# A factor for each position: spread over the partitions by a product, or read back from DRAM as one row

## The chip, the cores and the metric

The kernel runs on one core of a Trainium2 chip. Its engines are TensorE (PE in the profile, with PEld for its weight loads), VectorE (DVE), ScalarE (ACT) and GpSimd (POOL); SyncE (SP) issues most of the transfers. The metric is the device time of one launch in microseconds, lower is better.

## The reference

One layer of a hybrid block on x of 2048 positions by 1024 channels, in float32:

```python
h = rms_norm(x, norm1_g)                      # x * rsqrt(mean(x*x) + eps) * g
proj = h @ w_in                               # [u_a | v_a | val_b | gate_b], 512 columns each
u, v = gelu(u_a), layer_norm(gelu(v_a))
a = u * (tril(W_s[head]) @ v + b)             # within chunks of 128 positions
g = val_b * sigmoid(gate_b)
c = silu(group_layer_norm(causal_depthwise_conv31(g)))
x = x + concat([a, c]) @ w_out
f = square(relu(rms_norm(x, norm2_g) @ w_ff1))
x = x + f @ w_ff2
return rms_norm(x, final_g)
```

There are three root mean square norms. In each of them one factor per position, rsqrt(mean + eps), multiplies all 1024 channels of that position.

## The kernel before

**Layout.** Activations lie with channels on the 128 partitions and positions along the row: a piece of one block of 512 positions is a tile of 128 x 512, and eight such pieces are the 1024 channels. There are four blocks. Every large product is made as three (`mm3`): each float32 operand is split into a high part (rounded, by ACT: `h_hi`, `w_hi`, `fo_hi`) and a low part (the rest, by POOL or DVE: `h_lo`, `w_lo`, `fo_lo`), and hi x hi, hi x lo and lo x hi are added in one PSUM bank.

**Stages.** The order is "vgvgvgovgooo". `stage_v` makes the columns of u and v (`pvv`, `pu`) with their gating product (`sgu`); `stage_g` makes val and gate (`pv`, `pg`), and their `g<-pv,sg` starts a convolution on DVE: `conv_chain`, 31 steps `acc<-g,vec,acc` into PSUM, of which the last writes `c` into SBUF. `conv_tail` follows: PE transposes `c` (`ct`), DVE takes statistics of it (`st`, `mv`, `nb`, `ve`), POOL raises them to the power, ACT normalises, PE transposes back (`cb`). `stage_o` is the output projection (`po`). Then come the first layer of the MLP (`px`, `py`, `pz`; a Strassen-like set of seven products over blocks), the second (`py` with `fo` and `w2o`), 16 chunks for each pair of blocks, and the last norm with the output (`finish` for blocks 0 and 1, `finish_third`, `finish_last`).

**The factors.** The sum of squares of a block comes with positions on partitions, as a tile of 128 x 4 (`ss`), DVE adds eps (`ve`), and POOL raises to the power -1/2 (`r`, or `r1`). But the factors are needed as a row of 512, the same on all 128 partitions. `spread` makes that by a product. DVE multiplies the identity by `r`, which gives `dg`, four diagonal blocks side by side, and PE multiplies a matrix of ones by it, into a PSUM bank (`rbc`). The product has float32 operands and appears as two records in the trace. There are 13 of them:

- block 0's first norm (1), where the row is used after the projection;
- `make_h` for blocks 1 to 3 (3): DVE scales the eight pieces of the input `hf`, which SP loads, by gain and factor, reading the factor from the PSUM bank (`hf<-hf,vec,rbc`), then ACT and POOL split them. `make_h(b+1)` is a generator in the queue that `stage_g(b)` moves on by `tick`;
- `row_scale` for blocks 0 to 3, the second norm (4): one beat after the sums the power is taken, then `dg`, one beat later the product, one beat later ACT copies the bank into `r_rows`, a tile that the first MLP layer reads;
- `finish` for blocks 0 and 1 (2), eight DVE steps `x<-x,vec,rbc` with an output transfer each; one for the third block and two for the last.

**What sets the order.** The program is recorded by the Python code with clocks of its own (`dve.time`, `pe.time`); `background` puts convolution steps on DVE while its clock lags. `later(n, f)` calls f after n beats, a beat being half of an output column of `stage_o`. A scheduler then orders the instructions of the early stages, with pools whose buffers come free when the last reader has finished: `ct`, `cb`, `rbc`, `sgu` share the PSUM pool `tp`. `stage_o` and the MLP's first layer are kept in the written order. SP executes its queue in order, and so a transfer that waits holds those behind it.

Of the kernel before, what the change touches and what calls it, by code (L numbers as in the profile page):

```python
# [9 lines left out]
F32 = mybir.dt.float32  # L10
# [3 lines left out]
ALU = mybir.AluOpType  # L14

P = 128
# [3 lines left out]
TB = 512  # L20
KD = D // P
# [5 lines left out]
V_G1, V_G2, V_LNG, V_LNB, V_CB, V_CG, V_CBE = 0, 8, 16, 20, 24, 28, 32  # L27
V_FG = 36
# [54 lines left out]
def hybrid_block_kernel(  # L83
# [14 lines left out]
    nc = tc.nc  # L98
    dve = Clocked(nc.vector, lambda n: 0.35 if n <= 128 else 0.17 + n / 960.0)
    dcv = Clocked(nc.vector, lambda n: 0.15 + n / 960.0, dve.clock)  # L100
    dsb = Clocked(nc.vector, lambda n: 0.22 + n / 512.0 if n <= 512 else n / 640.0, dve.clock)
    gps = Clocked(nc.gpsimd, lambda n: 0.35 + n / 488.0 if n > 8 else 1.1)
    pe = Clocked(nc.tensor, lambda n: 0.0135 + n / 2400.0)
    pe4 = Clocked(nc.tensor, lambda n: 0.0135 + n / 600.0, pe.clock)
# [3 lines left out]
    dram = ctx.enter_context(tc.tile_pool(name="dram", bufs=1, space=bass.MemoryType.DRAM))  # L108
# [17 lines left out]

    p_d = dram.tile([2, 4, P, 2, TB], F32, name="p_d")
    x1_d = dram.tile([NB, 4, P, 1024], F32, name="x1_d")
    f_d = [dram.tile([8, 4, P, 2, TB], F32, name=f"f_d{i}") for i in range(2)]
    w2_d = dram.tile([8, 7, 2, P, 2, 512], F32, name="w2_d")  # L130
    w1_d = dram.tile([2, 7, P, 2, 512], F32, name="w1_d")
# [8 lines left out]
    def tmp(name, dtype=F32):  # L140
        return t2.tile([P, 512], dtype, tag="tmp", name=name)

    def bank(kind, name):
        return banks[kind].tile([P, 512], F32, tag=kind, name=name)

    def mm_tile(name):
        return bank("mm", name)

    def tp_tile(name):
        return bank("tp", name)  # L150

    def tiny(name, n=4):
        return small.tile([P, n], F32, tag=f"{name}{n}", name=name)

    def act_pair(name):
        return slot(f"{name}_hi", F32R), slot(f"{name}_lo", F32R)

    def split(src, hi, lo):

        nc.scalar.copy(hi, src)  # L160
        rest(src, hi, lo)
# [13 lines left out]
    def halves(pair):  # L175
        return [(pair[0][:, a * 512:a * 512 + 512], pair[1][:, a * 512:a * 512 + 512])
                for a in range(2)]
# [58 lines left out]
    ones = const.tile([P, P], F32, name="ones")  # L236
# [12 lines left out]
    def v(off, j):  # L249
        return vec[:, off + j:off + j + 1]  # L250

    def rsqrt(dst, src, mul):
        n = dst.shape[1]
        ve = tiny("ve")
        dve.tensor_scalar(ve[:, :n], src, mul, EPS, op0=ALU.mult, op1=ALU.add)
        gps.tensor_tensor(dst, ve[:, :n], nhalf.to_broadcast([P, n]), op=ALU.pow)
# [149 lines left out]
    def norm1(b, r):  # L406

        ss = tiny("ss")
        xin = []

        def load(i):
            xin.append(slot("xin"))
            nc.sync.dma_start(xin[i], x[(4 * b + i) * P:(4 * b + i + 1) * P, :])

        load(0)
        for i in range(4):
            if i < 3:
                load(i + 1)
            yield
            junk = t2.tile([P, 1024], BF16, tag="tmp", name="junk")  # L420
            nc.scalar.activation(junk, xin[i], AF.Square, accum_out=ss[:, i:i + 1])
        rsqrt(r, ss, 1.0 / D)

    def spread(r, ps):

        dg = tmp("dg")
        n = r.shape[1]
        dsb.tensor_tensor(
            dg.rearrange("p (n t) -> p n t", t=P)[:, :n, :],
            ident.unsqueeze(1).to_broadcast([P, n, P]),  # L430
            r.unsqueeze(2).to_broadcast([P, n, P]), op=ALU.mult)
        yield
        pe4.matmul(ps, ones, dg[:, :n * P], start=True, stop=True)

    def make_h(b, h):
        r = tiny("r1")
        yield from norm1(b, r)
        yield
        ps = tp_tile("rbc")
        yield from spread(r, ps)  # L440
        hf = []

        def load(k):
            hf.append(tmp("hf"))
            nc.sync.dma_start(hf[k], xt[b, k // 2, :, k % 2, :])

        load(0)
        for k in range(KD):
            if k < KD - 1:
                load(k + 1)  # L450
            yield
            if k % 2 == 0:
                pair = halves(act_pair("h"))
            dve.scalar_tensor_tensor(
                hf[k], hf[k], v(V_G1, k), ps, op0=ALU.mult, op1=ALU.mult)
            split(hf[k], *pair[k % 2])
            h.append(pair[k % 2])

# [31 lines left out]
    def feature_sums(acc, n, pc=None):  # L490

        pc = tp_tile("ssum") if pc is None else pc
        for i in range(n):
            for k, sq in enumerate(acc):
                pe4.matmul(pc[:, i:i + 1], sq[:, i * P:(i + 1) * P], ones[:, 0:1],
                           start=k == 0, stop=k == len(acc) - 1)
        return pc[:, :n]
# [100 lines left out]
    def later(n, f, first=False):  # L598
        due.append([n, f, first])
# [25 lines left out]
    def row_scale(b):  # L625

        r = r2[b]

        def spread_out():
            ps = tp_tile("rbc")  # L630
            g = spread(r, ps)
            next(g)

            def product():
                next(g, 0)
                later(1, lambda: nc.scalar.copy(r_rows[:, b % 2, :], ps))
            later(1, product)

        def sums():
            ps = feature_sums(acc[b], 4)  # L640
            later(1, lambda: rsqrt(r, ps, 1.0 / D))
            later(2, spread_out)
        return sums

    r_rows = const.tile([P, 2, TB], F32, name="r_rows")
# [40 lines left out]
    for kp in range(1, 4):  # L686
# [10 lines left out]
        out=wt, in_=wt, pattern=[[0, 4], [1, P]], compare_op=ALU.is_ge, fill=0.0,  # L697
# [47 lines left out]
    queue.append(make_cbias())  # L745
    late, rows0 = stage_v(0, h[0], parts[0], r0)
    queue.append(make_h(1, h[1]))
    stage_g(0, h[0], parts[0], late, rows0)
    drain()
    late, _ = stage_v(1, h[1], parts[1])  # L750
    queue.append(make_h(2, h[2]))
    slow.append(first_units())
    stage_g(1, h[1], parts[1], late)
    drain()
    late, _ = stage_v(2, h[2], parts[2])
    queue.append(split_mix(parts[0], mix[0]))
    queue.append(load_resids(0))
    stage_g(2, h[2], parts[2], late)
    drain()
    queue.append(make_h(3, h[3]))  # L760
    dve.time += BEHIND
    with tc.manual_schedule():
        stage_o(0, lambda d: tick(1))
    drain()
    late, _ = stage_v(3, h[3], parts[3])
# [212 lines left out]
    def up_out(pair):  # L978
        kept = {}

        def out(m, i, ps):
            blk_ = INTO[i]
            def copy():
                kept[m, blk_] = tmp("c")
                nc.scalar.copy(kept[m, blk_], ps)  # L985

            def finish():
                if i == 4:
                    src, c = ps, tmp("c")
                else:  # L990
                    c = kept.pop((m, blk_))
                    src = c if i == 7 else ps
                    dve.tensor_tensor(src, ps, c, op=ALU.add)
                (dsb if i == 7 else dve).scalar_tensor_tensor(
                    c, src, 0.0, r_rows[:, blk_[1], :], op0=ALU.max, op1=ALU.mult)
                later(1, lambda: nc.scalar.activation(c, c, AF.Square))  # L996
                later(2, lambda: nc.scalar.dma_start(
                    f_d[pair][m // 2, 2 * blk_[0] + blk_[1], :, m % 2, :], c))

            later(1, copy if i in (1, 5, 6) else finish, True)  # L1000
        return out
# [65 lines left out]
    with tc.manual_schedule():  # L1067
        stage_o(2, at_o2)
        pace["w2"] = 0.0
        k = w2st.at[2]  # L1070
# [4 lines left out]
    dn = {"x": [[] for _ in range(NB)]}  # L1075
# [53 lines left out]
    def finish(b, acc):  # L1129

        gaps = (6, 3, 4)
        for _ in range(gaps[0]):
            yield
        r = tiny("r1")
        ve = tiny("ve")
        ps = feature_sums(acc, 4, mm_tile("ssum"))
        yield
        dve.tensor_scalar(ve, ps, 1.0 / D, EPS, op0=ALU.mult, op1=ALU.add)
        gps.tensor_tensor(r, ve, nhalf.to_broadcast([P, 4]), op=ALU.pow)
        for _ in range(gaps[1]):  # L1140
            yield
        dg = tmp("dg")
        times_ident(dg, r)
        for _ in range(gaps[2]):
            yield
        ps = mm_tile("rbc3")
        pe4.matmul(ps, ones, dg, start=True, stop=True)
        x = dn["x"][b]
        for k in range(KD):
            yield  # L1150
            dve.scalar_tensor_tensor(x[k], x[k], v(V_FG, k), ps, op0=ALU.mult, op1=ALU.mult)
            nc.sync.dma_start(out[b, k // 2, :, k % 2, :], x[k])

    def times_ident(dg, r):
        dsb.tensor_tensor(
            dg.rearrange("p (n t) -> p n t", t=P), ident.unsqueeze(1).to_broadcast([P, 4, P]),
            r.unsqueeze(2).to_broadcast([P, 4, P]), op=ALU.mult)

    def gained(x, ks):
        for k in ks:  # L1160
            nc.scalar.activation(x[k], x[k], AF.Copy, scale=v(V_FG, k))
# [232 lines left out]
```

## Time and profile before

| | |
|---|---|
| median of 3 runs | 1819.01 us (1817.65 to 1820.26) |
| profiled execution | 1819.57 us |
| its span | 1817.8 us, mean granted clock 0.998 |
| PE busy | 1805.2 us, 99% |
| DVE busy | 1318.6 us, 73% |
| ACT busy | 754.6 us, 42% |
| POOL busy | 1232.4 us, 68% |

A row of the timeline has the start, the duration in us, the engine, the line and operation, the output and the inputs by their names, partitions x elements, and how many like it follow one another; in brackets stands the idle time before it and what ended that. The rows of L78 are those of a helper through which all DVE, POOL and PE operations are recorded, so they are told apart by the names of their tiles. Of three numbers in a row on a tile, the first to the third are the least, the median and the largest duration in ns.

### The profile page before, as it was taken

What the parts mean: (1) busy time and instruction counts of PE and PEld (TensorE: products, weight loads), DVE (VectorE), ACT (ScalarE), POOL (GpSimd) and SP (SyncE); (2) the same over time, 40 slices, a digit from 0 to 9 for tenths busy, and PEclk for the clock granted to TensorE, in tenths of its full rate; (3) what the DMA queues carried; (4) which work ended last, traced back from release to release, by engine and by line L of the source; (5) the groups of instructions that cost most, each with busy time, mean ns of one, the idle gap of its engine ahead of it and who ended that gap; (6) DMA issues with size and microseconds to landing.
All of it is one profiled execution on the core that took longest, in us unless ns stands there. A gap on an engine that the chain in (4) does not pass through costs nothing.

```text
span 1817.8 us, 23247 instructions
## 1 busy us (share of the span) xinstructions
PE 1805.2 (99%) x8080; PEld 1488.0 (82%) x8080; DVE 1318.6 (73%) x1832; ACT 754.6 (42%) x1170; POOL 1232.4 (68%) x788
## 2 busy tenths in 40 slices
PE   9999999999999999999999999999999999999998
PEld 7888888888888888888888888888888887888886
DVE  4699997996898985532667787787766678665565
ACT  6435556454454454455455555433212131222112
POOL 4575986884766666699778989786756464444434
PEclk9999999999999999999999999999999999999999
DMA  8353637442645464685557778999987679777752
GB/s 337 107 173 101 222 135 272 163 145 81 231 152 180 161 215 179 224 298 207 189 191 276 271 255 298 354 401 382 357 350 262 255 259 336 297 240 259 254 185 93
DMA packets 131686, 424.74 MB, mean 234 GB/s; under 512 B 14576, under 2 KB 15216, under 8 KB 131568
## 3 DMA queue, kind: packets, MB, share of 16 engines
q1 hardware_dynamic: 96000, 329.12, 50.7%
q10 hardware_dynamic: 35568, 94.13, 13.2%
q8 instruction: 64, 1.05, 0.2%
q14 instruction: 54, 0.44, 0.1%
HBM read 302.60 MB, written 120.59 MB: 233 GB/s over the span
## 4 chain that ended last, share of the span: by engine, by line
PE 92%; DVE 6%; issue 1%; POOL 1%; DMA 0%; ACT 0%; POOLq 0%; SPq 0%; DVEq 0%; ACTq 0%
PE py L78 51%; PE pz L78 9%; PE po L78 9%; PE px L78 5%; PE pv L78 4%; PE pg L78 4%; PE pu L78 4%; PE pvv L78 4%; DVE acc L78 3%; PE sgu L78 1%; PE rbc L78 0%; PE ssum L78 0%; DMA raw<-in_w_o 0%; PE cb L78 0%; PE ct L78 0%
## 5 line engine op out<-in xcount | busy, mean ns | idle before, releaser
L78 PE MATMUL py<-fo_hi,w2o 128*128 128x512 f32 x1792 | 555.1, 390 | 1.0 <-DVE x L78 1.0
L78 POOL TENSOR_TENSOR fo_lo<-fraw,fo_hi 128x1024 fp32r<-128x1024 f32 x112 | 283.0, 2535 | 260.6 <-ACT fo_hi L160 231.1
L78 DVE TENSOR_TENSOR x<-py,x 128x512 f32<-128x512 f32 x448 | 299.9, 687 | 175.4 <-PE py L78 175.2
L78 PEld LDWEIGHTS py<-fo_hi,w2o 128*128 128x128 f32 x1792 | 336.4, 188 | 71.6 <-DVE x L78 1.4
L78 PE MATMUL py<-hop,w1o 128*128 128x512 f32 x1536 | 363.6, 390 | 0.5 <-ACT c L985 0.5
L78 PE MATMUL py<-fo_lo,w2o 128*128 128x512 f32 x896 | 348.6, 389 | 0.0
L78 PEld LDWEIGHTS py<-hop,w1o 128*128 128x128 f32 x1536 | 287.7, 188 | 62.0 <-issue 1.3
L78 DVE SCALAR_TENSOR_TENSOR acc<-g,vec,acc 128x512 f32<-128x512 f32 x464 | 324.4, 750 | 1.9
L160 ACT CAST fo_hi<-fraw 128x1024 fp32r<-128x1024 f32 x112 | 116.9, 1052 | 424.7 <-PE py L78 209.7
L78 POOL TENSOR_TENSOR w_lo<-raw,w_hi 128x1024 fp32r<-128x1024 f32 (+1 forms) x94 | 224.1, 2390 | 61.4 <-ACT w_hi L160 50.9
L78 POOL TENSOR_TENSOR w1o<-wraw,w1o 128x512 fp32r<-128x512 f32 x120 | 172.9, 1446 | 51.9 <-ACT w1o L813 42.0
L78 PEld LDWEIGHTS py<-fo_lo,w2o 128*128 128x128 f32 x896 | 168.2, 188 | 35.6 <-issue 0.7
L78 PE MATMUL pz<-hop,w1o 128*128 128x512 f32 x768 | 183.8, 390 | 0.0
L78 POOL TENSOR_TENSOR w1o<-ws,w1o 128x512 fp32r<-128x512 f32 x90 | 128.9, 1435 | 65.4 <-ACT w1o L813 60.3
L78 PEld LDWEIGHTS pz<-hop,w1o 128*128 128x128 f32 x768 | 143.8, 188 | 29.7
L78 DVE TENSOR_TENSOR fraw<-fraw 128x1024 f32<-128x1024 f32 x64 | 92.1, 1439 | 16.3 <-POOL fo_lo L78 14.3
L996 ACT ACTIVATE c<-c 128x512 f32<-128x512 f32 x128 | 80.8, 632 | 54.8 <-DVE c L78 54.2
L78 PE MATMUL po<-m_hi,w_hi 128*128 128x512 f32 x256 | 101.1, 395 | 0.0
L78 PE MATMUL po<-m_hi,w_lo 128*128 128x512 f32 x256 | 99.9, 390 | 0.6 <-POOL w_lo L78 0.6
L78 PE MATMUL po<-m_lo,w_hi 128*128 128x512 f32 x256 | 99.7, 389 | 0.0
L78 DVE TENSOR_TENSOR px<-px,c 128x512 f32<-128x512 f32 x32 | 22.4, 699 | 102.3 <-PE px L78 69.0
L78 POOL TENSOR_TENSOR w2p<-wraw,w2p 128x512 fp32r<-128x512 f32 x64 | 92.6, 1447 | 2.6 <-ACT w2p L813 2.6
(157 smaller groups left out, 2928.4 us busy)
## 6 DMA issues: line engine op xcount, KB each, us to landing
w2o<-w_d SPq DMA_DIRECT2D x224, 512.0 KB, 6.2
w_d<-w2p ACTq DMA_DIRECT2D x112, 512.0 KB, 5.0
wraw<-in_w SPq DMA_DIRECT2D x92, 512.0 KB, 4.6
f_d<-c ACTq DMA_DIRECT2D x128, 256.0 KB, 4.0
fraw<-f_d SPq DMA_DIRECT2D x64, 512.0 KB, 6.7
raw<-in_w_ct SPq DMA_DIRECT2D x48, 512.0 KB, 5.2
raw<-in_w_o SPq DMA_DIRECT2D x32, 512.0 KB, 5.9
w1o<-w_d SPq DMA_DIRECT2D x28, 512.0 KB, 5.5
```

Of the source, the lines that this page charges most:

```text
L78: return op(out, *args, **kwargs)
L160: nc.scalar.copy(hi, src)
L996: later(1, lambda: nc.scalar.activation(c, c, AF.Square))
```

## The change

Nine of the thirteen products, those of `make_h`, `row_scale` and `finish`, are replaced by two transfers on SP's queue: `write_factor` puts `r` (128 x 4 floats) into a row of 512 in DRAM, and `read_factor` reads this row back to all 128 partitions (256 KB). `make_h` and `finish` read the result from an SBUF tile `rows`, `row_scale` reads straight into `r_rows`. In `finish`, POOL multiplies two of the eight pieces, to which ACT gave the gain first, and the output transfers are issued two steps later.

```diff
+    r_d = dram.tile([9, 4, P], F32, name="r_d")
...
+    def write_factor(n, r):
+        nc.sync.dma_start(r_d[n].rearrange("n p -> p n"), r)
+
+    def read_factor(n, rows):
+        nc.sync.dma_start(rows, r_d[n].rearrange("n p -> (n p)").unsqueeze(0).to_broadcast([P, TB]))
...
     def make_h(b, h):
         r = tiny("r1")
         yield from norm1(b, r)
         yield
-        ps = tp_tile("rbc")
-        yield from spread(r, ps)
+        write_factor(5 + b, r)
+        yield
+        rows = tmp("rows")
+        read_factor(5 + b, rows)
         hf = []
...
             dve.scalar_tensor_tensor(
-                hf[k], hf[k], v(V_G1, k), ps, op0=ALU.mult, op1=ALU.mult)
+                hf[k], hf[k], v(V_G1, k), rows, op0=ALU.mult, op1=ALU.mult)
...
     def row_scale(b):
-        def spread_out():
-            ps = tp_tile("rbc")
-            g = spread(r, ps)
-            next(g)
-
-            def product():
-                next(g, 0)
-                later(1, lambda: nc.scalar.copy(r_rows[:, b % 2, :], ps))
-            later(1, product)
-
         def sums():
             ps = feature_sums(acc[b], 4)
             later(1, lambda: rsqrt(r, ps, 1.0 / D))
-            later(2, spread_out)
+            later(2, lambda: write_factor(b, r))
+            later(4, lambda: read_factor(b, r_rows[:, b % 2, :]))
         return sums
...
     def finish(b, acc):
...
-        dg = tmp("dg")
-        times_ident(dg, r)
+        write_factor(4 + b, r)
+        gained(dn["x"][b], (0,2))
+        for _ in range(gaps[1]):
+            yield
+        rows = tmp("rows")
+        read_factor(4 + b, rows)
         for _ in range(gaps[2]):
             yield
-        ps = mm_tile("rbc3")
-        pe4.matmul(ps, ones, dg, start=True, stop=True)
         x = dn["x"][b]
-        for k in range(KD):
+        for k in range(KD + 2):
             yield
-            dve.scalar_tensor_tensor(x[k], x[k], v(V_FG, k), ps, op0=ALU.mult, op1=ALU.mult)
-            nc.sync.dma_start(out[b, k // 2, :, k % 2, :], x[k])
+            if k in (0,2):
+                gps.tensor_tensor(x[k], x[k], rows, op=ALU.mult)
+            elif k < KD:
+                dve.scalar_tensor_tensor(
+                    x[k], x[k], v(V_FG, k), rows, op0=ALU.mult, op1=ALU.mult)
+            if k > 1:
+                nc.sync.dma_start(out[b, k // 2 - 1, :, k % 2, :], x[k - 2])
```

The scheduler lays out the early stages anew. Three places are shown. The first is DVE while block 1's `stage_g` runs, around the last step (`c`) of one convolution; `mv`, `nb`, `ve` are the statistics of an earlier one, `hf` are block 2's inputs. Before, with the eighth `hf` behind that `c`:

```order
L78 SCALAR_TENSOR_TENSOR acc<-g,vec,acc 128x512
L78 BN_AGGR mv<-st 128x2 x3
L78 TENSOR_TENSOR g<-pv,sg 128x512
L78 BN_AGGR mv<-st 128x2
L78 SCALAR_TENSOR_TENSOR acc<-g,vec,acc 128x512 x2
L78 TENSOR_SCALAR nb<-mv 128x4
L78 TENSOR_SCALAR ve<-mv 128x4
L78 SCALAR_TENSOR_TENSOR acc<-g,vec,acc 128x512
L78 SCALAR_TENSOR_TENSOR c<-g,vec,acc 128x512
L78 SCALAR_TENSOR_TENSOR acc<-g,vec,acc 128x512
L78 TENSOR_SCALAR acc<-g,vec 128x512
L78 SCALAR_TENSOR_TENSOR hf<-hf,vec,rbc 128x512
```

After, on the same engine, from the third of the new `hf` steps to that same `c`:

```order
L78 SCALAR_TENSOR_TENSOR hf<-hf,vec,rows 128x512 x2
L78 SCALAR_TENSOR_TENSOR acc<-g,vec,acc 128x512
L78 SCALAR_TENSOR_TENSOR hf<-hf,vec,rows 128x512 x2
L78 TENSOR_TENSOR g<-pv,sg 128x512
L78 SCALAR_TENSOR_TENSOR acc<-g,vec,acc 128x512
L78 SCALAR_TENSOR_TENSOR hf<-hf,vec,rows 128x512
L78 SCALAR_TENSOR_TENSOR acc<-g,vec,acc 128x512 x6
L78 SCALAR_TENSOR_TENSOR hf<-hf,vec,rows 128x512
L78 SCALAR_TENSOR_TENSOR c<-g,vec,acc 128x512
```

All eight `hf` steps of the block now stand ahead of this `c`, the first two of them just above these rows; before, seven did. Counted over the stretch from the `g` ahead of the norm (at 171.10 us in the profile) to that `c`, 25 operations of 128 x 512 and a `dg` have become 29 and none.

PE at the start of `stage_v` for block 2, where `ct` are the transposes of that `c`. Before, they stand among the later `pvv` products:

```order
L78 MATMUL pvv<-w_hi,h_hi 128x512 x4
L78 MATMUL cb<-ident,c 128x128 x4
L78 MATMUL ct<-ident,c 128x128 x4
L78 MATMUL pvv<-w_lo,h_hi 128x512
L78 MATMUL pvv<-w_hi,h_lo 128x512
```

After, they follow the first three:

```order
L78 MATMUL pv<-h_hi,w_lo 128x512
L78 MATMUL pvv<-w_hi,h_hi 128x512 x3
L78 MATMUL ct<-ident,c 128x128 x4
L78 MATMUL pvv<-w_lo,h_hi 128x512
L78 MATMUL pvv<-w_hi,h_lo 128x512
```

They moved forward by some 75 products. On SP, around the same norm, before:

```order
L445 DMA hf<-in_xt 128x512 x3
L743 DMA w_d<-w1o 128x1024
L445 DMA hf<-in_xt 128x512 x4
L206 DMA raw<-in_w_v 128x1024 x2
L743 DMA w_d<-w1o 128x1024
```

and after:

```order
L438 DMA r_d<-r_1403 128x4x1
L745 DMA w_d<-w1o 128x1024
L442 DMA rows<-r_d 128x512
L456 DMA hf<-in_xt 128x512 x7
L207 DMA raw<-in_w_v 128x1024 x2
```

The three `hf` loads that stood ahead of a write of MLP weights (`w_d<-w1o`) now stand behind it and behind the factor's way through DRAM.

## The prediction

> **What bounds the kernel now.** I read the page first: the busy times, the slices, and the chain that ended last.
>
> ```profile
> span 1817.8 us, 23247 instructions
> PE 1805.2 (99%) x8080; PEld 1488.0 (82%) x8080; DVE 1318.6 (73%) x1832; ACT 754.6 (42%) x1170; POOL 1232.4 (68%) x788
> ...
> DVE  4699997996898985532667787787766678665565
> ...
> POOL 4575986884766666699778989786756464444434
> ...
> PE 92%; DVE 6%; issue 1%; POOL 1%; DMA 0%; ACT 0%; POOLq 0%; SPq 0%; DVEq 0%; ACTq 0%
> ```
>
> PE is busy 99% of the span and makes 92% of the chain. So a product that leaves PE shortens the run by its own length, unless PE then waits for somebody. The candidate stands in the slices: one slice is 45 us, and in slices 3 to 6 DVE is at 90% and more, with POOL at 50 to 90%. The windows of block 2's norm and of what follows it, and the chain in them, show who leads there:
>
> ```profile
> 171.00:198.00 27.00, 27.00 (x123) 22.05 (x122) 26.90 (x43) 13.81 (x21) 21.14 (x18) 1.00 0.72 238
> 198.00:259.00 61.00, 60.02 (x280) 49.33 (x278) 60.57 (x96) 38.46 (x55) 59.26 (x42) 1.00 0.53 191
> ...
> 198.31 17.12 DVE acc L78 x26
> ...
> 220.31 5.35 DVE nb L78
> ...
> 258.36 0.60 DVE u L78
> 259.10 1.13 PE sgu L78 x8
> ```
>
> Columns of a window are its length, then the busy times of PE, PEld, DVE, ACT and POOL. DVE is busy 87.47 of 88 us, and the chain runs on DVE until the `sgu` product at 259.10. Whatever DVE is given or spared between 171 and 259 us reaches the end one for one. Elsewhere PE leads.
>
> **The nine products.** What one of them costs PE is read from a pair of neighbours in block 3's norm, against the usual step of 24 products in 5.44 us, 0.227 us each:
>
> ```profile
> 89.80 5.44 PE pg L78 x24
> ...
> 303.98 0.40 PE L78 MATMUL po<-m_hi,w_lo 128*128 128x512 f32 x1
> 304.21 1.02 PE L78 MATMUL rbc<-dg,ones 128*128 128x512 f32 x2
> 304.67 0.80 PE L78 MATMUL po<-m_hi,w_hi 128*128 128x512 f32 x1
> 305.31 0.40 PE L78 MATMUL po<-m_lo,w_hi 128*128 128x512 f32 x1
> ...
> L78 PE MATMUL rbc<-dg,ones x26: 592/592/1069, 35.2 to 1809.5; 128*128 128x512 f32 x26
> ```
>
> From 303.98 to 305.31 are 1.33 us for two `po` steps and one `rbc` (two records): 1.33 - 2 x 0.227 = 0.874. The tile has 26 records, 13 products; block 0's, the third's and the last's two stay, so nine go: 9 x 0.874 = **-7.87 us**. The four ACT copies of `row_scale` go too, but no row has PE waiting for ACT there: zero.
>
> **Block 2's first norm.** The factor is now read from SBUF, where before it came from PSUM. The same operation stands in the trace in both forms (ns, least, median and most):
>
> ```profile
> L78 DVE SCALAR_TENSOR_TENSOR hf<-hf,vec,rbc x24: 733/744/748, 83.3 to 320.0; 128x512 f32<-128x512 f32 x24
> L78 DVE SCALAR_TENSOR_TENSOR c<-c,r_rows x32: 691/694/2708, 503.8 to 1174.2; 128x512 f32<-128x512 f32 x32
> L78 DVE SCALAR_TENSOR_TENSOR c<-c,r_rows 128x512 f32<-128x512 f32 x32 | 33.3, 1040 | 1.3
> L78 DVE SCALAR_TENSOR_TENSOR xr<-xr,vec 128x512 f32<-128x512 f32 x24 | 28.6, 1207 | 25.3 <-POOL hop L78 25.0
> 171.71 2.23 DVE L78 TENSOR_TENSOR dg<-ident,r 128x512 f32<-128x512 f32 x1
> ...
> 170.98 2.40 POOL L78 TENSOR_TENSOR w_lo<-raw,w_hi 128x1024 fp32r<-128x1024 f32 x1
> ```
>
> With one operand in PSUM the step takes 733 to 748 ns, never more; with both in SBUF it goes from 691 to 2708 ns, and its mean is 1040. The last two rows show why: `dg`, with both operands in SBUF, starts at 171.71 and is held until 173.9, just after POOL's `w_lo` ends at 173.38. DVE waits out whatever POOL has running.
>
> By the Trainium skill (SBUF — State Buffer, the rule on the shared port pair) the lock is exclusive for a whole instruction and the loser blocks. The trace agrees, in the 2.23 above. The rule speaks against this change: by it each `hf` step that finds POOL at work pays, and the eight of block 2 alone bring the sum from 1811.6 to 1816.8; by the row of 733 to 748 ns they would stay free.
>
> The price of one step therefore lies between 0 (POOL idle) and 2.4 (a whole `w_lo`); the two means give 1.04 - 0.69 = 0.35 and, against the old step, 1.207 - 0.744 = 0.46. POOL is busier here, 21.14 of 27 us, with pieces of 1.3 and 2.4 us. Its share, 0.78, times half a piece (0.65 to 1.2) is 0.5 to 0.9; I take 0.65, near the lower end and the means: 8 x 0.65 = **+5.2 us** on DVE. Of this DVE gives back the `dg` that is gone, **-2.2**.
>
> ```profile
> 170.00 1.01 POOL L78 TENSOR_TENSOR r<-ve,nhalf 128x4 f32<-128x4 f32 x1
> 175.11 0.33 SPq L743 DMA_DIRECT2D w_d<-w1o  x1
> p_d<-u SPq DMA_DIRECT2D x8, 256.0 KB, 2.4
> hf<-in_xt SPq DMA_DIRECT2D x24, 256.0 KB, 5.0
> wt<-in_sgu_wt SPq DMA_DIRECT2D x1, 256.0 KB, 9.8
> ```
>
> Then the factor's way. `r` is there at 171.0, and the 2 KB write follows on SP. Nothing in the trace writes single numbers; the nearest write to DRAM, `p_d<-u`, lands in 2.4 us, and the nearest row with 512 short pieces, the load `wt`, in 9.8. I take 2.4 (a write, and little data) and keep 9.8 for a rival. On SP `w_d<-w1o` stands between write and read, and it goes at 175.11, so the read is issued at 175.4 and lands, by the `hf` row, by 180.4 at the latest. All `hf` loads now stand behind the read, 0.4 us each, the first landing near 180.8 at that 5.0, or 178.3 at the 2.4. DVE has eight operations of 0.66 us and 1.5 us of small statistics between 171.7 and its first `hf`, and arrives near 178.5. It waits 0 to 2.3 us, taken as **+1.0**. In this window the saved product (0.874 at 177.5) only lets PE arrive sooner at the same DVE: **+0.87** back. Together: 5.2 - 2.2 + 1.0 + 0.87 = 4.9.
>
> ```profile
> 171.10 0.69 DVE L78 TENSOR_TENSOR g<-pv,sg 128x512 f32<-128x512 f32 x1 [0.15 <-PE pv L78]
> ...
> 189.95 2.45 DVE L78 TENSOR_SCALAR ve<-mv 128x4 f32<-128x4 f32 x1
> ...
> 192.97 0.73 DVE L78 SCALAR_TENSOR_TENSOR c<-g,vec,acc 128x512 f32<-128x512 f32 x1
> ...
> 194.47 0.84 PE L78 MATMUL pvv<-w_hi,h_hi 128*128 128x512 f32 x3
> ...
> 181.31 2.56 POOL L78 TENSOR_TENSOR h_lo<-hf,h_hi 128x512 fp32r<-128x512 f32 x2 [5.80 <-ACT h_hi L160]
> ```
>
> Where PE will feel it first is told by the order: the transposes of this `c` (`ct`) came some 75 products behind the start of `pvv`, and now stand right behind its first three. From `g` at 171.10 to the end of `c` were 22.5 us; four more 0.66 us operations now stand in between (2.6) and no `dg` (-2.2), one of two contended `nb`/`ve` like the 2.45 above may go (-1.4), seven contended `hf` come (+4.6) and the wait (+1.0): `c` ends near 193.6 + 4.6 = 198.2. PE is there at 194.47 + 3 x 0.227 - 0.87 = 194.3. So the 4.9 show as a stall of about 4 us at `ct`, the rest at `sgu`. There PE's list is shorter by 7.4 us ahead of the product and DVE's by 6.05 ahead of `u` (counted from the order by these durations), another **+1.3**, at most 1.3 and perhaps nothing.
>
> **Blocks 1 and 3.** Block 3's `hf` fall into 297 to 325 us, where DVE is busy 17.55 of 28 us: hidden, and 10 us of cover. Block 1's fall where it has little:
>
> ```profile
> 76.00:119.00 43.00, 43.00 (x191) 35.22 (x190) 41.23 (x63) 16.31 (x21) 34.90 (x26) 1.00 0.46 147
> 297.00:325.00 28.00, 28.00 (x125) 22.84 (x124) 17.55 (x28) 15.95 (x26) 22.02 (x17) 1.00 0.43 153
> ```
>
> 8 x 0.65 = 5.2, less a `dg` of about 2.2, is 3 us more for a DVE with 1.8 us idle: 0 to 2 us, since PE takes the `g` of this stretch some time after DVE has it; taken **+0.5**.
>
> **Second norm (four products).** Write at beat 2, read at beat 4, straight into `r_rows`. Block 1 is the tightest:
>
> ```profile
> 491.45 1.02 POOL L78 TENSOR_TENSOR r<-ve,nhalf 128x4 f32<-128x4 f32 x1 [1.36 <-DVE ve L78]
> 503.80 1.21 DVE L78 SCALAR_TENSOR_TENSOR c<-c,r_rows 128x512 f32<-128x512 f32 x1
> ```
>
> `r` at 492.5, write 2.4, two beats or the write's landing, read 2.4 to 5.0: near 500.5, some 3 us ahead of the use at 503.80. Zero; the form of the reader does not change, it read SBUF before.
>
> **Last norm of blocks 0 and 1.** Here the eight steps stood in one batch, and PE waited behind it:
>
> ```profile
> 1493.90 2.90 DVE L78 TENSOR_TENSOR dg<-ident,r 128x512 f32<-128x512 f32 x1 [0.28 <-POOL r L78]
> 1503.10 5.34 DVE L78 SCALAR_TENSOR_TENSOR x<-x,vec,rbc 128x512 f32<-128x512 f32 x8
> 1508.49 0.50 PE L78 MATMUL py<-fo_hi,w2o 128*128 128x512 f32 x1 [0.97 <-DVE x L78]
> ```
>
> Now POOL takes two of the eight, and `dg` is gone. The 0.97 should go: **-1.0**. Six contended steps of 0.35 to 0.65 (2 to 4 us) come on DVE, which has 27% of the span free; that is no reason for a new stall except within the batch, where 2 steps less (1.3 us) stand against it: -1.0 to +1.
>
> **The sum.** -7.87 + 4.9 + 1.3 + 0.5 - 1.0 = -2.2 us. The profiled execution took 1819.57, so 1817.4 for it; the median of the runs is 0.56 below, which gives **1816.8 us**. A run agrees to about 3.6 us (0.2%) with no change, so this is called the same.
>
> **Rivals.**
> - *The contention doesn't reach PE* (faster). For it: POOL stood idle for 5.80 us up to 181.31, just where the new `hf` steps begin, `nb` alone cost 5.35 in the chain and can come out shorter with other timing, and PE has other work. Against it: DVE busy 26.90 of 27. Then -7.87 - 1.0 remain: 1810.1; with a lost half of the 4.9, 1812.6.
> - *The 2 KB write lands late* (slower). 512 pieces of 4 bytes, like `wt` at 9.8: 7.4 later, SP holds the `hf` loads behind the read and DVE the conv behind the first `hf`. At block 2 7.4 more, less at most 1 of slack, 6.4; at `r_rows` 7.4 - 3 = 4.4, where DVE holds the banks of the products behind it. 1816.8 + 10.8 = 1827.6. It decides (over 1822.6) from 5.8 / 2 = 2.9 us beyond the 2.4, near 5.5. For it: 9.8 is the only row with so many pieces; against it: that load ran at the crowded start, with 128 times the data.
> - By the Trainium skill (DMA: Bandwidth & Descriptors, its rules for kernel authors) a last dimension that isn't contiguous is one descriptor per element, and below 512 B a write is a read and a write. No trace here shows such a write; by that rule the late landing is this rival's.
>
> **Chances.** Forecast (between 1815.4 and 1822.6) 0.46; contention that doesn't reach PE 0.42, all of it faster; late write and worse stalls 0.12. So faster 0.42, within 0.2% 0.46, slower 0.12. The forecast's own range is 1814 to 1821. The whole range goes from 1809 (all saved, and another microsecond of the stalls gone) to 1823, where the late write begins.
>
> **What would show it.** Right: 8 records of `rbc` instead of 26; `hf` at a mean of 1.2 to 1.5 us; a PE wait for `c` of 3 to 5 us shortly after 194; no wait at 1507; the write's landing below 4 us. Wrong: `hf` near 0.75 (the first rival), or a first `hf` that waits several microseconds for the DMA of `rows` (the second). A PE that waits at a place not named here would upset the sum altogether.

## The result, and the profile after

| | before | after |
|---|---|---|
| median | 1819.06 us (1817.65 to 1820.26) | 1872.33 us (1870.5 to 1874.94) |
| span of the profiled execution | 1817.8 us | 1868.8 us |
| mean granted clock | 0.998 | 0.987 |

The ratio is 1.0295, with an interval of 1.0282 to 1.0307: 53.3 us slower, where no change was forecast. One run of e5 (2935 us) and one of g1 (4288 us) in the experiments below lie far above the others of their kernels, and the medians given there leave them out, while the 1837.2 in g1b's expectation counts it. The page of the kernel after, with the lines that answer to those of before:

```profile
span 1868.8 us, 23258 instructions
PE 1813.7 (97%) x8062; PEld 1492.0 (80%) x8062; DVE 1316.0 (70%) x1820; ACT 754.5 (40%) x1170; POOL 1244.7 (67%) x791
...
PEclk9999899999999999999999999999999998899999
...
PE 84%; DMA 5%; DVE 4%; issue 3%; POOL 3%; ACT 1%; SPq 0%; POOLq 0%; DVEq 0%; ACTq 0%
```

DMA, which was at 0% of the chain, now has 5%. The chain of waits, in order of time, names it (start, us, what):

```profile
76.16 7.94 DMA r_d<-r
84.58 6.15 DMA hf<-in_xt
...
180.64 10.20 DMA r_d<-r
191.26 4.99 DMA hf<-in_xt
...
319.38 7.93 DMA r_d<-r
329.18 7.57 DMA hf<-in_xt
...
1526.18 10.24 DMA r_d<-r
1536.48 4.70 DMA rows<-r_d
...
1572.82 8.15 DMA r_d<-r
1581.40 7.03 DMA fraw<-f_d
```

Five of the nine factors stand in the chain: those of the first norm (blocks 1, 2 and 3) and of the last norm (block 1 comes first, then block 0). Each time it is the write of 2 KB, 8 to 10 us from its issue to the next step, and then a load of 5 to 8 that stands behind it on SP. The list of transfers (KB, and median us from issue to landing) and DVE's list of waits (us in all, times, the longest) say the same:

```profile
hf<-in_xt SPq DMA_DIRECT2D x24, 256.0 KB, 6.5
...
rows<-r_d SPq DMA_DIRECT2D x5, 256.0 KB, 5.9
...
r_d<-r SPq DMA_DIRECT2D x9, 2.0 KB, 8.2
```

```profile
DVE hf L78 <- DMA hf<-in_xt: 28.9, 4, 12.6
...
DVE x L78 <- DMA rows<-r_d: 15.1, 2, 8.2
...
DVE c L78 <- DMA r_rows<-r_d: 10.8, 2, 5.5
```

How one of them reaches PE is seen in the last norm of block 1, in the timelines of DVE and PE:

```profile
1541.20 6.17 DVE L78 SCALAR_TENSOR_TENSOR x<-x,vec,rows 128x512 f32<-128x512 f32 x6 [6.91 <-DMA rows<-r_d]
```

```profile
1537.90 0.62 PE L78 MATMUL py<-fo_hi,w2o 128*128 128x512 f32 x2
1538.36 0.39 PE L78 MATMUL py<-fo_lo,w2o 128*128 128x512 f32 x1
1548.03 0.80 PE L78 MATMUL py<-fo_hi,w2o 128*128 128x512 f32 x1 [9.28 <-DVE x L78]
```

DVE comes to the six steps and waits 6.91 us for the row; the additions `x<-py,x` stand behind them on the same engine, no PSUM bank comes free, and PE stops from 1538.8 to 1548.0. The windows (length, busy us of PE, PEld, DVE, ACT, POOL, then the granted clock) show that the stop costs more than its length:

```profile
1538.00:1548.00 10.00, 0.74 (x4) 0.28 (x2) 6.80 (x8) 0.00 (x0) 2.93 (x2) 0.73 0.80 226
1548.00:1553.00 5.00, 4.97 (x12) 3.92 (x13) 4.15 (x7) 1.04 (x1) 0.00 (x0) 0.51 1.05 375
1553.00:1563.00 10.00, 10.00 (x46) 8.27 (x45) 7.17 (x9) 1.46 (x2) 5.18 (x2) 1.00 1.02 397
```

For 5 us after it the clock is 0.51 and 12 products are done where 22 go at full speed.

Where the 53 us arise was worked out from the starts of the same product in both traces (the n-th of its name). PE is late by 8.7 us after block 1's first norm, by 20.9 at 195 us of before's time and 19.4 at 290, 28.0 after block 3's (328 us), 30.2 at 398, 32.1 at 1490, 40.4 after the first last norm and 50.7 after the second and at the end. So the three first norms cost some 30 us, the two last norms 19, and the four second norms together 2, all with the saved products counted.

### The profile page after: what moved, and what is told of

It reads as the page before. It is cut to its first block, busy times and chain, and to the rows that moved or that the text cites. A ratio compares the mean times of both kernels' runs of the same rounds, so it can differ in the third digit from the quotient of the medians.

```text
span 1868.8 us, 23258 instructions
## 1 busy us (share of the span) xinstructions
PE 1813.7 (97%) x8062; PEld 1492.0 (80%) x8062; DVE 1316.0 (70%) x1820; ACT 754.5 (40%) x1170; POOL 1244.7 (67%) x791
## 4 chain that ended last, share of the span: by engine, by line
PE 84%; DMA 5%; DVE 4%; issue 3%; POOL 3%; ACT 1%; SPq 0%; POOLq 0%; DVEq 0%; ACTq 0%
PE py L78 48%; PE pz L78 9%; PE po L78 7%; PE pvv L78 5%; PE px L78 5%; PE pu L78 4%; PE pg L78 3%; DMA r_d<-r 2%; PE pv L78 2%; DVE acc L78 1%; DVE hf L78 1%; POOL w_lo L78 1%; DMA hf<-in_xt 1%; POOL hop L78 1%; PE sgu L78 1%
## 5 line engine op out<-in xcount | busy, mean ns | idle before, releaser
L78 POOL TENSOR_TENSOR w_lo<-raw,w_hi 128x1024 fp32r<-128x1024 f32 (+1 forms) x94 | 224.4, 2394 | 70.6 <-ACT w_hi L161 60.9
L78 DVE TENSOR_TENSOR fraw<-fraw 128x1024 f32<-128x1024 f32 x64 | 96.0, 1499 | 12.7 <-POOL fo_lo L78 12.7
```

What stands on the lines that cost most here:

```text
L78: return op(out, *args, **kwargs)
```

## The experiments

**Each part alone.** Each of the three kernels is the one before with one part of the diff above: `row_scale`, `finish` or `make_h`, with `write_factor` and `read_factor`.

> Only the four factors of the second norm go through DRAM; the first norm and the last go by the product as before. Theory A: four products less (-3.5 us), and at most 2 us of waiting at each of the two tight blocks: 1815 to 1820 us. Theory B: the same, since r_rows was in SBUF before, 1815.5. If above 1825, the second norm has a part in the 53 us that the lateness of PE did not show.

> Only the last norm's factor of blocks 0 and 1 goes through DRAM. Theory A: two stalls of 10 us each, as in the changed kernel's trace near 1540 and 1590 us, less two products: 1836 to 1842 us. Theory B: twelve steps with a second SBUF operand, with POOL a third busy here: 1817 to 1821 us.

> Only the three factors of the first norm go through DRAM, 4 byte pieces. Theory D: 30 us, the lateness that PE had at the end of that part in the changed kernel: 1845 to 1852 us. Together with e4 (+21.9) this would be nearly the whole. If the three parts simply add, 53 - 22 - 7 = 24: 1843.

| kernel | median | to the kernel before |
|---|---|---|
| e3_only_row_scale | 1826.19 us | 1.0042 (1.0027 to 1.0057) |
| e4_only_finish | 1840.68 us | 1.0124 (1.0107 to 1.0141) |
| g4_only_make_h | 1850.81 us | 1.0174 (1.0160 to 1.0188) |

That is +7.4, +21.9 and +31.6 us. The last norm and the first are what the trace said, and within what was expected. The second norm alone was expected to gain and loses 7.4: DVE's waits in it name `r_rows<-r_d` (12.3 us, twice, up to 6.4). Together the three make 60.9, not 53.3: in company each costs less (30, 2 and 19 by PE's lateness), the second norm above all. Why was not tested.

**Is it the wait for the write?** The write stays, and the read takes a row of 512 times 0.5 that is written once at the start, so the nine factors are left out of the result. With nothing to wait for, the scheduler also puts the reads and some of their uses elsewhere.

```diff
+    old_d = dram.tile([4, P], F32, name="old_d")
...
-        nc.sync.dma_start(rows, r_d[n].rearrange("n p -> (n p)").unsqueeze(0).to_broadcast([P, TB]))
+        nc.sync.dma_start(rows, old_d.rearrange("n p -> (n p)").unsqueeze(0).to_broadcast([P, TB]))
```

> The nine writes stay, but each read takes another row, of 512 times 0.5, written once at the start (the norms then multiply by that): nothing waits for a write of factors any more, and the number of multiplications is the same. Theory A, the write lands late and the rest queues behind it: the 53 us vanish but for what the forecast had summed, 1811 to 1820 us. Theory B, the second SBUF operand is what costs (24 hf steps that wait for POOL): most of it stays, above 1855 us. Theory C, SP's order (hf loads now behind the read) costs by itself: some 10 us stay for each make_h, 1835 to 1850.

1861.91 us, 1.0236 (1.0221 to 1.0252): a miss for theory A in this form. Only 10 us went. Nothing waited for a factor's write any more, and yet 43 stayed. The number lies in theory B's range, but the second operand by itself costs far less (g3 below). The transfers of this kernel show what else was there:

```profile
hf<-in_xt SPq DMA_DIRECT2D x24, 256.0 KB, 9.3
...
rows<-old_d SPq DMA_DIRECT2D x5, 256.0 KB, 9.2
...
r_rows<-old_d SPq DMA_DIRECT2D x4, 256.0 KB, 14.3
...
r_d<-r SPq DMA_DIRECT2D x9, 2.0 KB, 10.2
```

Loads that depend on nothing took 9 to 14 us. So a new theory, D: the write is slow, and it holds up the transfers that are issued after it.

**What makes the write slow.** A chain of single transfers behind the end of the kernel before, each waiting for the one ahead, of which the first three are:

```diff
+            q.dma_start(ma.rearrange("n p -> p n"), seed)
+            ra = tmp("ra")
+            q.dma_start(ra, ma.rearrange("n p -> (n p)").unsqueeze(0).to_broadcast([P, TB]))
+            q.dma_start(mb, ra[:, :4])
```

> The kernel before, with a chain of single transfers behind its end, three times over, each waiting for the one before: writes of 512 x 4 bytes (as in the change), 512 x 4 bytes set 128 bytes apart, 128 x 4, 128 x 16, 4 x 512, 1 x 2048 and 128 x 2048 bytes, each read back. Theory A1, the landing grows with the number of small pieces: 512 x 4 bytes near 7 us, 128 pieces 2.5 to 3.5, one piece 2. Theory A2, any small write is late whatever its number: 128 x 4 and 128 x 16 near 7 too. Theory A3, only the crowded queue makes it late: all at 2 to 3 us here. Neighbours in one DRAM line as the cause: 512 pieces 128 bytes apart land much sooner than 512 side by side.

SP's timeline of the second of three rounds; a write's landing is the step from its own row to the next one:

```profile
1863.10 0.37 SPq L1358 DMA_DIRECT2D ma_d<-seed  x1
1874.22 0.32 SPq L1360 DMA_DIRECT2D ra<-ma_d  x1
1877.27 0.32 SPq L1362 DMA_DIRECT2D mb_d<-ra  x1
1878.67 0.32 SPq L1364 DMA_DIRECT2D rb<-mb_d  x1
1881.26 0.32 SPq L1366 DMA_DIRECT2D mc_d<-rb  x1
1888.65 0.32 SPq L1368 DMA_DIRECT2D rc<-mc_d  x1
1893.43 0.37 SPq L1370 DMA_DIRECT2D me_d<-rc  x1
1895.91 0.37 SPq L1372 DMA_DIRECT2D re<-me_d  x1
```

| write | tile | us, three rounds |
|---|---|---|
| 512 x 4 bytes side by side (the change) | `ma` | 13.2, 11.1, 8.7 |
| 128 x 4 bytes side by side | `mc` | 7.0, 7.4, 8.0 |
| 512 x 4 bytes, 128 bytes apart | `me` | 1.9, 2.5, 2.2 |
| 128 x 16 bytes side by side | `mb` | 2.6, 1.4, 1.4 |
| 4 x 512 bytes | `mh` | 1.2, 1.2, 1.2 |
| 1 x 2048 bytes | `mf` | 1.2, 1.2, 1.2 |
| 128 x 2048 bytes | `mg` | 2.1, 2.0, 2.0 |

Neither the number of pieces (A1), nor their smallness (A2), nor a crowded queue (A3) makes it slow, but 4 byte pieces that are neighbours in DRAM. Sizes between 4 and 16 bytes were not tried, and why neighbours hinder one another no run here shows.

**Does it hold up others?** e5 is e1 with another layout of `r_d` and nothing else; k1 and k2 add the nine writes, unread, to the kernel before. Within each pair the instructions and their order on every engine are the same.

```diff
-    r_d = dram.tile([9, 4, P], F32, name="r_d")
+    r_d = dram.tile([9, 4, P, 32], F32, name="r_d")
...
-        nc.sync.dma_start(r_d[n].rearrange("n p -> p n"), r)
+        nc.sync.dma_start(r_d[n][:, :, 0].rearrange("n p -> p n"), r)
```

> Like e1_old_row in every instruction and in their order (reads of a row of 512 times 0.5), only that the nine writes put their 512 numbers 128 bytes apart in DRAM instead of side by side. Theory D, numbers side by side make the write slow (8.7 to 13.2 us alone, 1.9 to 2.5 when set apart) and it holds up the transfers behind it on the same engines: e1's 43 us above the kernel before go almost wholly, 1812 to 1822 us. Theory B, the second SBUF operand: unchanged, 1855 to 1865.

> The kernel before, with all its products, and in addition the nine writes of the change, which nobody reads. Theory D, the write holds up the transfers behind it: the loads that PE needs come 7 us later, 1825 to 1845 us. Theory F, only the wait for the row costs: 1818 to 1821 us.

> As k1, the same instructions in the same order, with the 512 pieces of each write 128 bytes apart in DRAM. Theory D: 1818 to 1821 us, and the difference to k1 is the price of the hold-up. Theory F: the same as k1.

| kernel | median | to the kernel before |
|---|---|---|
| e1, side by side | 1861.91 us | 1.0236 (1.0221 to 1.0252) |
| e5, apart | 1833.21 us | 1.0079 (1.0062 to 1.0096) |
| k1, side by side, unread | 1836.01 us | 1.0094 (1.0080 to 1.0108) |
| k2, apart, unread | 1819.45 us | 1.0001 (0.9992 to 1.0010) |

The layout alone is worth 28.7 us in the first pair and 16.6 in the second. e5 stays above the range that D gave. Its 14.4 us arise in two places, which only e1 and e5 have in this form; between them PE wins back 2.7. In the first 32 us of the kernel the extra row is written and read (PE is late by 8.8 us at 32 us). At the last norms the uses of the row in both blocks now come nearly in one stretch on DVE, ahead of the additions, and PE's lateness goes from 6.1 to 14.7 us:

```profile
1506.69 5.25 DVE L78 SCALAR_TENSOR_TENSOR x<-x,vec,rows 128x512 f32<-128x512 f32 x3 [0.28 <-DMA rows<-old_d]
1511.86 0.68 DVE L78 TENSOR_TENSOR x<-py,x 128x512 f32<-128x512 f32 x1
1512.46 8.56 DVE L78 SCALAR_TENSOR_TENSOR x<-x,vec,rows 128x512 f32<-128x512 f32 x9
```

In the clean pair, k1 and k2, the list of transfers shows the hold-up, k1 ahead of k2 (us from issue to landing, least, median and most, of the `hf` loads behind the writes):

```profile
DMA to landing us min/median/max: 3.8/12.1/14.3
```

```profile
DMA to landing us min/median/max: 3.5/5.0/7.0
```

Loads that have nothing to do with the write land 7 us later when it stands ahead of them in this layout, and 17 us of the kernel's time go that way with no reader at all. Single packets show it too: in k1 37 packets of 2 or 4 KB took more than 5 us each, up to 10.4, and in k2 none more than 2.2.

**The second SBUF operand.**

```diff
         yield from spread(r, ps)
+        rows = tmp("rows")
+        nc.scalar.copy(rows, ps)
...
-                hf[k], hf[k], v(V_G1, k), ps, op0=ALU.mult, op1=ALU.mult)
+                hf[k], hf[k], v(V_G1, k), rows, op0=ALU.mult, op1=ALU.mult)
```

> The kernel before with its product; only in the first norm ACT copies the bank of factors into SBUF and the 24 hf steps read the copy. This is the price of the second SBUF operand and nothing else. The sum of the prediction: 8 x 0.65 us in block 2 and 0.5 in block 1, 1822 to 1826 us. If it is hidden: 1818 to 1820. If it is the main cost of the change (theory B): above 1840.

1827.32 us, 1.0045 (1.0029 to 1.0060), +8.2, just above the 1822 to 1826 that were expected. The groups and PE's waits of this kernel:

```profile
L78 DVE SCALAR_TENSOR_TENSOR hf<-hf,vec,rows 128x512 f32<-128x512 f32 x24 | 32.1, 1349 | 2.9 <-ACT rows L442 2.9
```

```profile
PE pvv L78 <- DVE g L78: 6.7, 2, 5.6
```

1349 against 743 ns: 0.61 us a step, where 0.65 was taken; and PE stops at block 2's start for 5.6. The copy on ACT is in the 8.2 too: DVE waits 2.9 us for it, where it waited 2.0 for the product. The mechanism and nearly its size were right. In this kernel the transposes `ct` do not stand behind the first three `pvv` products, so the stop comes at `g`. In the changed kernel PE does stop at `ct`, as the prediction had it, though there the late `hf` loads have a part in it:

```profile
215.31 1.11 PE L78 MATMUL ct<-ident,c 128*128 128x128 f32 x4 [4.33 <-DVE c L78]
```

**A quick write.** f1, f2 and f3 write 16 byte pieces and read the row with a stride of four; h4 turns `r` on PE first.

```diff
-    r_d = dram.tile([9, 4, P], F32, name="r_d")
+    r_d = dram.tile([9, P, 4], F32, name="r_d")
...
-        nc.sync.dma_start(r_d[n].rearrange("n p -> p n"), r)
+        nc.sync.dma_start(r_d[n], r)
...
+    def turned(rows):
+        return rows.rearrange("p (q n) -> p n q", n=4)
```

> The whole change, with the factor written as 128 pieces of 16 bytes (alone 1.4 to 2.6 us), and the row read back in the order in which it then lies; the multiplications read it with a stride of four. Theory D: the time of the sum in the prediction, 1812 to 1822 us, of which what is above 1811 is the price of the second SBUF operand and of the 5 us that a read takes. Theory B: above 1850. Theory E, the round trip through DRAM is too long whatever the write (5 us for the read remain, and the hf loads still stand behind it): 1825 to 1840.

> The last norm of blocks 0 and 1 alone through DRAM, with 16 byte pieces. Theory D: two products less and the old wait of 1 us gone, 1815 to 1818 us, against 1840.7 with 4 byte pieces. Theory E: a wait of 3 to 5 us for the row stays at each, 1822 to 1828.

> The second norm alone through DRAM, with 16 byte pieces. Theory D: four products less and no wait, 1814 to 1817 us, against 1826.2 with 4 byte pieces. Theory E: 1818 to 1822. If it stays at 1826, the waits of that norm come from the read or from the order, not from the write.

```diff
+    def turn(r, pt):
+        pe4.matmul(pt[0:4, :P], r, ident, start=True, stop=True)
+        rt = tmp("rt")[0:4, :P]
+        nc.scalar.copy(rt, pt[0:4, :P])
+        return rt
...
-        write_factor(5 + b, r)
+        write_factor(5 + b, turn(r, tp_tile("rt")))
```

> The whole change, all nine factors, with PE's small turn, ACT's copy and a write of four pieces of 512 bytes; rows and their use as in the change. If the slow write is at the root of both the hold-up (17 us in k1) and most of the wait for the rows: what stays is the second SBUF operand (g3, +8.4), the read's 5 us at the places with no slack, some 3 us at a turn that waits for r, less nine times 0.65: 1822 to 1832 us. If waiting for a read of 5 us costs as much as the whole round trip did: above 1845.

| kernel | median | to the kernel before |
|---|---|---|
| f1, all nine | 1853.00 us | 1.0194 (1.0177 to 1.0211) |
| f2, last norm | 1830.23 us | 1.0065 (1.0050 to 1.0080) |
| f3, second norm | 1827.31 us | 1.0048 (1.0033 to 1.0063) |
| h4, all nine, turned on PE | 1837.56 us | 1.0110 (1.0093 to 1.0126) |

The f runs have a second effect in them, which their expectations had left out. The group of f1, against 691 ns before:

```profile
L78 DVE SCALAR_TENSOR_TENSOR c<-px,r_rows 128x512 f32<-128x512 f32 x32 | 34.3, 1071 | 1.1
```

Reading the row with a stride of 16 bytes lengthens each step by 0.38 us, and the 128 such steps of the MLP give back what was won: in f3 PE is 1.8 us ahead at 497 us, then falls back all through the MLP's first layer, and is 8.3 behind at the end, while DVE waits for no row. So where f1 lands in theory B's range and f3 near the 1826 it names, the stride explains it as well, f2 misses both of its ranges, and the three tell little of D. (The Trainium skill, SBUF — State Buffer, in the section Door 1: The DMA port swizzle, says that accesses pay for each new line of 16 bytes; the 0.38 us agree.) h4 has neither stride nor slow write: of the 53 us 34 go. Its 19.3 that stay were expected at 4 to 14. PE is late by 13.8 us after the first norms and by 13.0 at 1490, and 4.2 more come in the last norm, where PE waits 2.9 us for `r` at its turn. In block 3's first norm DVE still waits 8.9 us for a first `hf`, and PE loses 5.6:

```profile
319.88 0.75 DVE L78 SCALAR_TENSOR_TENSOR hf<-hf,vec,rows 128x512 f32<-128x512 f32 x1 [8.88 <-DMA hf<-in_xt]
```

So the order on SP, with the `hf` loads behind the factor's transfers (theory C of e1), has a part in what stays. How the rest of it divides was not measured.

**A later use.**

```diff
-        for _ in range(gaps[2]):
+        for _ in range(gaps[2] + 10):
```

> As e4_only_finish (the last norm of blocks 0 and 1 through DRAM, 4 byte pieces), with ten more steps of some 1.4 us between the read and the use in the code. In the scheduler's order this moves block 1's steps six additions further back, block 0's stay where they were, as a control. Theory F, the loss is DVE standing in order at a row that isn't there yet: block 0 stalls as in e4 (10.5 us), block 1 no longer does (10 us less): 1829 to 1833 us. Theory G, the slow write also holds up the weights behind it, so PE stops wherever the use stands: 1838 to 1842.

> The kernel of g1 once more, for its trace: it took 1837.2 us, 3.5 less than e4. Of the two last norms the one that comes first (block 1's) has its use in the old place, the second (block 0's) six additions later. Theory F: PE's wait of some 9 us stays at the first and is gone or below 6 us at the second.

1836.07 us (1.0096, 1.0081 to 1.0112) and, once more, 1838.94 (1.0110, 1.0092 to 1.0129). The expectation of g1 has the two blocks exchanged. It is a miss: in g1b's trace DVE still waits 9.06 us at the first and 9.63 at the second, because the second write moved along with its use (issued at 1551.89, and DVE stands at the use 3.7 us later, until 1565.18; in e4 it came there after 5.6 us). A use that is truly later behind the slow write wasn't tried, and so the wait's share isn't measured by itself.

**A version that gains?** `turn` again, in h3 for the second norm alone, in h2 also for block 1's last norm.

```diff
-            later(2, spread_out)
+            later(2, lambda: write_factor(b, turn(r, tp_tile("rt"))))
+            later(4, lambda: read_factor(b, r_rows[:, b % 2, :]))
```

> First norm, and last norm of block 0, by the product as before. For the second norm and the last norm of block 1, PE turns r (128 x 4) into 4 x 128 with one product of 128 columns (some 0.2 us in place of 0.87), ACT copies it, and the write is four pieces of 512 bytes (1.2 us alone); the row is read back as in the change, and block 1's use stands six steps later. Five products cheaper by 0.65 us, and block 1's old wait: -3 to -4 us, 1815 to 1816 us, if no row is late. If the rows are still late (theory E, the read's 5 us), 1818 to 1824.

> Only the second norm through DRAM, by PE's small turn and four pieces of 512 bytes; the first norm and the last by the product. In h2's trace PE was 1.98 us ahead at 898 us, after the four, and lost 3 at the turn in the last norm, which this kernel doesn't have: 1816.5 to 1818 us.

h2 took 1820.40 us (1.0010, 1.0001 to 1.0019), not the 1815 to 1816 that were expected, h3 1817.89 (0.9994, 0.9985 to 1.0003), as expected. In h2 PE was 1.98 us ahead after the second norm, and then it waited for its own turn in the last norm:

```profile
1492.17 0.38 PE L78 MATMUL rt<-ident,r 128*4 128x128 f32 x2 [2.83 <-POOL r L78]
```

h3, without that, ends with PE 1.7 us ahead. In both some 0.4 to 0.6 us of the lead are there at 30 us, ahead of every change; what is left is some 0.3 us for each of the four products. It is within what a measurement of this kernel can tell from nothing.

## Why the prediction was wrong

- **The step that failed** is the landing of the write, in the part on block 2: "I take 2.4 (a write, and little data) and keep 9.8 for a rival." It took 8.2 in the median and 10.2 at that place. The other end, 9.8, was the right one, but for the wrong cause: 512 pieces set apart land in 2.2.
- **The rival was too cheap.** The late write was there, with a chance of 0.12, at 1827.6 us. It charged 6.4 us at block 2 and 4.4 at `r_rows`. At block 2 that was about right: 4.9, 1.3 and 6.4 make 12.6, and PE's lateness grew there from 8.2 at 171 us to 19.4 at 290, by 11.2. Two things were missing. It charged nothing to block 1 (8.7), nothing to block 3 ("10 us of cover"; PE lost 9.5, since DVE stood 12.6 us at the first `hf`) and nothing to the last norms, for which the part on them never asked when the row would be there (19 us). And it took the write for one late transfer, while it makes others late too (17 us in k1). Where it would decide was misjudged as well: with its own slack of 1 and 3 us it passes 1822.6 at a landing of 7.3 us, not near 5.5; the measured 8.2 lies above both.
- **Products saved:** 0.874 for each (by its own figures 0.876) agrees with e4: PE's lead grows from 0.70 to 1.60 us at 1497, where the first of the two products stood, and before its row is used.
- **Second operand:** 0.61 us a step against 0.65, and 8.2 us in all against the 7.0 of the terms that belong to it (5.2 and 1.3 in block 2, 0.5 in block 1). Right in kind and nearly in size, in the order of the kernel before.
- **The signs.** Of those that the prediction named for being right, three came in the changed kernel: 8 records of `rbc`, `hf` at a mean of 1.395 us, and the wait of 4.33 for `c`. Two did not: PE still stops near 1507 (in before's time), and the write lands far above 4 us.
- **The old wait of 1 us at 1507** went, but one product later PE stopped for 9.28.
- **Second norm:** the row was to be "some 3 us ahead of the use" in block 1; in e3 DVE waited 5.9 us for it there. In the changed kernel PE lost 2 us from 398 to 1490 although four products (3.5) were gone, so the waits there cost some 5 where the forecast had zero.
- **By the Trainium skill** (DMA: Bandwidth & Descriptors, its table of specifications) transfers below 512 bytes pay by a read and a write. That pointed to the slow write, but the runs put the border elsewhere: pieces of 16 bytes land in 1.4 us and single numbers apart in 2.2; only neighbouring numbers take 7.0 to 13.2. By the measurement the rule's size is not the cause here.

How the 53.3 us divide is known in part. The hold-up is 16.6 us in the order of the kernel before (k1 against k2) and 28.7 in the order of e1 and e5. The second operand is 8.2 in the order of before (g3). In the changed order it may be less: in e5, which reads SBUF too, PE's lateness grew only from 8.8 us at 32 us to 9.4 at 398, with three products saved. The nine products are -7.9 by the prediction's price. What is left, some 24 to 36 us by which hold-up is taken, is a remainder and not a measurement: DVE standing in order at rows and `hf` loads that aren't there, with PE's half clock after each stop. h4 shows it from the other side: 34 of the 53 go with the slow write. The parts do not add strictly, as e3, e4 and g4 show.

## What to carry to other kernels

A tiny transfer is not a cheap one: ask of a write in which pieces it reaches DRAM and what is queued behind it, before comparing it with work on a busy engine. Where the trace has no such transfer, the two nearest rows are the ends of a range, and each place that waits for it has to be charged with both ends, also those that seem to have cover. One engine that executes in order turns a late row into a stop of everything behind it.

## What the runs showed of the hardware

- 4 byte writes side by side in DRAM: 8.7 to 13.2 us for 512, 7 to 8 for 128, 1.9 to 2.5 for 512 that lie 128 bytes apart, 1.4 to 2.6 for 128 of 16 bytes (e2, one transfer at a time).
- Such a write delays loads behind it on its queue: `hf` takes 12.1 us in k1 and 5.0 in k2, where the numbers lie apart.
- After a stop of PE of 9.3 us the granted clock was 0.51 over the next 5 us. The Trainium skill (TensorE: Matmul & The Clock Gate, its part 1) tells of a half clock after an idle window; the trace agrees.
- A step of DVE on 512 numbers with one operand at a stride of 16 bytes takes 1.07 us in place of 0.69 (f1).
